# A hybrid attention block: local keys and latents projected transposed, as three pairs of column tiles by seven half-size products

## The chip, the cores and the metric

The kernel runs on one core of a Trainium2 chip. The metric is the device time of one execution in microseconds (us). The engines are PE (matrix products), DVE (element-wise on vectors), ACT (functions, casts and copies), POOL (a further element-wise engine) and SP, which issues most DMA transfers. Each engine works through its own queue in order; semaphores hold an instruction until another engine's result is there. Everything is float32 in and out; products are made in a reduced float32 form, with each operand split into a high and a low part.

## The reference

Per layer (there is one), for 1024 tokens of width 1024:

```python
h  = RMSNorm(x)
p  = h @ w_in    # [SWA q 512 | SWA k 128 | SWA v 128 | q-latent 384 | kv-latent 256 | rope-key 32 | two gates 2048]
A  = sliding_window_attention(rope(q), rope(k), v)        # 8 heads of 64, 2 key heads, window 128
cq, ckv = RMSNorm(q_latent), RMSNorm(kv_latent)
B  = mla_attention(cq @ w_uq, ckv @ w_ukv, rope(rope_key))  # 8 heads, 64 + 32 columns, causal
y  = sigmoid(gate_a) * (A @ w_o_swa) + sigmoid(gate_b) * (B @ w_o_mla)
x  = x + y @ w_out
x  = x + (silu(n @ w_gate) * (n @ w_up)) @ w_down,  n = RMSNorm(x)
return RMSNorm(x)
```

## The kernel before

**Products.** A product of float32 accuracy is three matmuls: high x high, low x high, high x low (`mm3`, L168 to L174). `split` (L161 to L166) makes the parts: ACT casts the high part, DVE subtracts it from the source.

**The normalised input h** comes in blocks of 128 tokens, transposed (`xt`), and is split into four quadrants `hh`, `hl`: two halves of the 1024 features by two halves of the tokens. Each block is also stored to `h_d` in DRAM.

**Projections by block.** For each of eight blocks of tokens there are these products with h as the stationary side: `kvq` (L515), 512 columns: half of the local queries, the local keys, the local values; `qa` (`q_first`, L504), 256 columns: the other half of the queries; later `ql`, 416 columns: the query latents and the rope key; and `kl`, 256 columns: the key-value latents. Rope is applied to queries and keys by `rope_nat` on DVE. Keys must be transposed for the attention: `k_twice`, `k_transposes` (L488) and `k_split` (L497) do it by PE, ACT and DVE. The latents are normalised by row as they come out (`latent_end` L748, `kv_out` L1032), stored to `lat_d`, loaded again behind the local attention (`load_lat` L1076) and transposed there by PE (`latent_T` L1115, forty transposes of 128x128).

**The gates by seven products.** The 2048 gate columns are made by the class `Seven` (L762): two column tiles of 128 by two halves of the tokens by two halves of the features is a 2x2 matrix product, done with seven products of half size (twelve matmuls of 512 columns each) in place of eight. Such products take sums: of the weights (`mix` L802, on POOL in pieces, six operations per pair; plus two for product 7) and of h, called `t1` to `t4`. `set_of_h` (L710) makes these sums for 128 columns of either half of the tokens: loads `hr` and `ht` from `h_d`, DVE does `hr`, POOL `ht` (two operations), DVE `ht` of the other half, ACT and DVE the three splits, and POOL the raw `t4` (two operations, `h`). `prep` (L816) splits the weights of a product, `prep_to` runs it ahead.

**The order.** PE and SP follow the order of the program throughout; up to the local attention ACT, DVE and POOL do too. There the program first interleaves `kvq` and `qa` of the blocks with the normalising of the next, then runs the eight `ql`, beside which the four sets of h are made, then the eight `kl`, beside which the first gate pair is mixed and the `t4` parts are split; then the sixteen steps of local attention with three gate products each. Behind them come the last gate products, the `lT` transposes, and the up-projections `k` and `q` of the latents, for whose weights `uq` and `ukv` are loaded and split there. On-chip buffers are of two kinds of slots, `u` (21) and `v` (17): a tile's transfer waits until the slot's last reader is done.

Of the kernel before, what the change touches and what calls it, by code (L numbers as in the profile page):

```python
# [17 lines left out]
P = 128  # L18
# [24 lines left out]
C_RT = QL  # L43
C_CKV = QL + ROPE_B
LAT = C_CKV + KVL
# [44 lines left out]
def hybrid_block_kernel(  # L90
# [6 lines left out]
    w_qa: bass.AP,  # L97
    w_ql: bass.AP,
    w_kl: bass.AP,
    w_gt: bass.AP,  # L100
    sinks: bass.AP,
    q_g: bass.AP,
    w_uq: bass.AP,
    kv_g: bass.AP,
# [10 lines left out]
    c_rope_b: bass.AP,  # L115
    c_rope_t: bass.AP,
# [80 lines left out]
    rp1 = const.tile([P, 64], F32, name="rp1")  # L197
# [14 lines left out]
    lat_d = dram.tile([NB, P, LAT], F32, name="lat_d")  # L212
# [214 lines left out]
    khd = []  # L427
    for g in range(NG):
        t = V("khd", F32R, (P, 2, S))
        khd.append((t[:, 0], t[:, 1]))  # L430
# [3 lines left out]
    def rope_nat(ps, heads, hw, cos, sin, outs, r=None):  # L434
        n = heads * 2 * hw
        t = U("rp") if heads > 1 else rp1
# [24 lines left out]
    wqa = []  # L461
    kvq_ps, qns, sums, q_ps = {}, {}, {}, {}
# [25 lines left out]
    def k_transposes(b):  # L488
        qn = qns.pop(b)
        nc.sync.dma_start(q_d[NB + b], qn[:, 0:256])  # L490
        pt = kT_ps[b] = P1("kT", (P, NG, P))
        for g in range(NG):
            nc.tensor.transpose(pt[:, g], qn[:, 512 + P * g:512 + P * (g + 1)], ident)

    kT_ps = {}

    def k_split(b):  # L497
        pt = kT_ps.pop(b)
        for g in range(NG):
            nc.scalar.copy(khd[g][0][:, blk(b)], pt[:, g])  # L500
        for g in range(NG):
            sub(khd[g][1][:, blk(b)], pt[:, g], khd[g][0][:, blk(b)].bitcast(F32), nc.vector)

    def q_first(b, mid=None):  # L504
        ps = q_ps[b] = P1("qa", (P, 256))
# [29 lines left out]

    def rope_kvq(b):
        ps = kvq_ps[b]
        r = rn[:, b:b + 1]
        v_hi, v_lo = vv[b // 4][:, b % 4, :, 0:HD], vv[b // 4][:, b % 4, :, HD:P]
        v_ps = ps[:, 384:512].rearrange("p (g d) -> p g d", g=NG)  # L540
        if b < RAW:
            nc.scalar.activation(v_hi, v_ps, AF.Copy, scale=r)
        else:
            nc.scalar.copy(v_hi, v_ps)
        qns[b] = rope_of(ps[:, 0:384], 6, b, r if b < RAW else None)
        if b < RAW:
            nc.vector.scalar_tensor_tensor(v_lo, v_ps, r, v_hi.bitcast(F32), op0=ALU.mult, op1=ALU.subtract)
        else:
            nc.vector.tensor_tensor(v_lo, v_ps, v_hi.bitcast(F32), op=ALU.subtract)
        kvq_ps.pop(b)  # L550

    def k_twice(b):
# [34 lines left out]
    square(1)  # L587
    kvq(2)
    load_xt(5)
    load_xs(5)  # L590
    load_xs(4)
    load_xt(6)
    rope_kvq(0)
    to_quad(3)
    k_twice(0)
    rope_kvq(1)
    to_quad(4)
    square(2)
    k_twice(1)
# [1512 lines left out]
```

## Time and profile before

| | |
|---|---|
| Times of three runs | 1321.82, 1321.95, 1324.46 us (median 1321.95) |
| Span of the profiled execution | 1323.3 us, 19060 instructions |
| Its own time beside the median | 1.35 us above (the span is the only time shown for it) |
| Granted TensorE clock | 9 of 9 in all 40 slices |
| DMA | 245.12 MB, mean 185 GB/s |

A row of a timeline has the start in us, the duration in us (of several alike: from the first start to the last end), engine, line, operation, output <- inputs, shape and count, and in brackets how long the engine had been idle and what ended that. Matmuls are pipelined, so a row's duration is longer than the step from one start to the next; the step is what a stream of them costs.

### The profile page before, as it was taken

How to read it: one execution, taken by the hardware profiler on the slowest of the kernel's cores; microseconds unless marked ns; L12 is line 12 of the kernel's file. 1: busy time of each engine (PE TensorE's matmuls, PEld its weight loads, DVE VectorE, ACT ScalarE, POOL GpSimd, SP SyncE). 2: the span in 40 equal slices, each digit the busy share in tenths (PEclk: the TensorE clock that was granted, in tenths of full speed). 3: DMA queues.
4: the chain of work that ended last, by engine and by line, in shares of the span. 5: the costliest groups of instructions: out<-in, count | busy, mean ns of one | idle time of the engine just before them, and what ended most of it. 6: DMA issues, size and time to landing. Idle time of an engine off the chain costs nothing.

```text
span 1323.3 us, 19060 instructions
## 1 busy us (share of the span) xinstructions
PE 1310.9 (99%) x6516; PEld 1103.7 (83%) x6516; DVE 917.0 (69%) x1517; ACT 634.6 (48%) x1282; POOL 559.0 (42%) x619
## 2 busy tenths in 40 slices
PE   9999999999999999999999999999999999999997
PEld 6899888888888889888888888888888888888886
DVE  6868787786767777777779655656666554664863
ACT  7444667665557666755355232323222223644452
POOL 1116545653324556312232465777567631022521
PEclk9999999999999999999999999999999999999999
DMA  9464344456577477898531334655544435996504
GB/s 359 167 195 154 125 162 145 140 184 212 166 241 201 97 223 160 277 322 195 181 122 48 112 130 172 235 195 206 183 181 148 150 112 198 378 376 224 175 17 142
DMA packets 92192, 245.12 MB, mean 185 GB/s; under 512 B 10304, under 2 KB 17984, under 8 KB 90944
## 3 DMA queue, kind: packets, MB, share of 16 engines
q1 hardware_dynamic: 87264, 233.15, 50.9%
q0 software_dynamic: 3392, 8.39, 3.6%
q10 hardware_dynamic: 1440, 2.36, 0.5%
q8 instruction: 52, 0.85, 0.3%
q14 instruction: 44, 0.36, 0.1%
HBM read 161.16 MB, written 78.51 MB: 181 GB/s over the span
## 4 chain that ended last, share of the span: by engine, by line
PE 63%; DVE 2%; issue 1%; POOL 1%; ACT 1%; POOLq 0%; DVEq 0%; ACTq 0%
PE fa L174 6%; PE fa L172 6%; PE fa L173 6%; PE fd L173 5%; PE fd L172 5%; PE fd L174 5%; PE fb L173 5%; PE fb L174 5%; PE fb L172 5%; PE xo L174 2%; PE xo L172 2%; PE xo L173 2%; PE pTb L1280 1%; PE oB L174 1%; PE oB L172 1%
## 5 line engine op out<-in xcount | busy, mean ns | idle before, releaser
L166 DVE TENSOR_TENSOR wl<-wr,wl 128x512 fp32r<-128x512 f32 x150 | 142.5, 973 | 74.7 <-ACT wl L163 74.2
L166 DVE TENSOR_TENSOR lrv<-lr,lrv 128x1024 fp32r<-128x1024 f32 x77 | 105.5, 1401 | 48.2 <-ACT lrv L163 45.6
L163 ACT CAST lrv<-lr 128x1024 fp32r<-128x1024 f32 x77 | 80.2, 1054 | 90.4 <-PE fd L174 56.7
L172 PE MATMUL fd<-lrv 128*128 128x512 f32 x308 | 119.8, 389 | 0.0
L173 PE MATMUL fd<-lrv 128*128 128x512 f32 x308 | 119.8, 389 | 0.0
L174 PE MATMUL fd<-lrv 128*128 128x512 f32 x308 | 119.8, 389 | 0.0
L177 POOL TENSOR_TENSOR wr<-wr,sm 128x512 f32<-128x512 f32 (+1 forms) x38 | 45.5, 1208 | 139.9 <-DVE wl L166 121.7
L163 ACT CAST wl<-wr 128x512 fp32r<-128x512 f32 x150 | 86.7, 621 | 4.8 <-DVE t3l L177 2.8
L166 DVE TENSOR_TENSOR wl<-sm,wl 128x512 fp32r<-128x512 f32 x60 | 50.2, 859 | 42.1 <-ACT wl L163 41.9
L1265 POOL TENSOR_TENSOR denb<-denb,neg_one 128x1 f32<-128x1 f32 x64 | 39.8, 622 | 92.7 <-ACT p L1264 80.7
L172 PEld LDWEIGHTS fd<-lrv 128*128 128x128 f32 x308 | 57.8, 188 | 12.1
L174 PEld LDWEIGHTS fd<-lrv 128*128 128x128 f32 x308 | 57.8, 188 | 12.0
L173 PEld LDWEIGHTS fd<-lrv 128*128 128x128 f32 x308 | 57.8, 188 | 11.9
L1264 ACT ACTIVATE p<-scb,nmb 128x384 f32<-128x384 f32 (+3 forms) x64 | 47.7, 746 | 32.0 <-DVE nmb L1263 23.5
L361 POOL TENSOR_SCALAR ms<-ss 128x1 f32<-128x1 f32 x32 | 8.9, 278 | 125.9 <-ACT xn L1742 47.5
L1263 DVE CUSTOM_DVE_ANT_0 scb<-scb,mask 128x384 f32<-128x384 f32 (+3 forms) x64 | 48.5, 761 | 17.2 <-PE scb L1255 14.6
L1638 ACT ACTIVATE act<-sm 128x512 f32<-128x512 f32 x11 | 7.0, 635 | 102.1 <-DVE sm L180 102.1
L166 DVE TENSOR_TENSOR ptl<-pTb,pth 128x512 fp32r<-128x512 f32 (+2 forms) x96 | 50.0, 550 | 7.9 <-ACT pth L163 7.7
L163 ACT CAST pth<-pTb 128x512 fp32r<-128x512 f32 (+2 forms) x96 | 43.4, 480 | 18.1 <-PE pTb L1280 17.1
L1266 POOL TENSOR_SCALAR p<-p,denb 128x384 f32<-128x384 f32 (+3 forms) x64 | 48.2, 753 | 6.3
L172 PE MATMUL fa<-t1h,wl 128*128 128x512 f32 x120 | 47.1, 392 | 0.4 <-ACT wl L163 0.4
L172 PE MATMUL fb<-t2h,wl 128*128 128x512 f32 x120 | 47.1, 392 | 0.0
(357 smaller groups left out, 4260.7 us busy)
## 6 DMA issues: line engine op xcount, KB each, us to landing
lr<-la_d SPq DMA_DIRECT2D x77, 256.0 KB, 5.4
wr<-in_w_gate_dram SPq DMA_DIRECT2D x22, 512.0 KB, 4.3
wr<-in_w_up_dram SPq DMA_DIRECT2D x22, 512.0 KB, 5.0
la_d<-sd SPq DMA_DIRECT2D x22, 512.0 KB, 5.2
wd<-in_w_down_dram SPq DMA_DIRECT2D x22, 512.0 KB, 6.6
rb_d<-wd SPq DMA_DIRECT2D x22, 512.0 KB, 2.7
lr<-rb_d SPq DMA_DIRECT2D x44, 256.0 KB, 5.4
lr<-in_w_down_dram SPq DMA_DIRECT2D x33, 256.0 KB, 5.4
```

The lines of the kernel that those rows point to most:

```text
L163: i = nc.scalar.copy(hi, src)
L166: (eng or nc.vector).tensor_tensor(lo, src, hi.bitcast(F32), op=ALU.subtract)
L172: nc.tensor.matmul(ps, ah, bh, start=first and i == 0, stop=False, skip_group_check=go_on)
L173: nc.tensor.matmul(ps, ah, bl, start=False, stop=False, skip_group_check=go_on)
L174: nc.tensor.matmul(ps, al, bh, start=False, stop=last and i == n - 1, skip_group_check=go_on)
L177: eng.tensor_tensor(out, a, b, op=ALU.subtract)
L361: nc.gpsimd.tensor_scalar(ms, ss, 1.0 / width, EPS, op0=ALU.mult, op1=ALU.add)
L1263: nc.vector.tensor_tensor_reduce(s_, s_, m_, 1.0, -NEG, op0=ALU.add, op1=ALU.min, accum_out=nm)
L1264: nc.scalar.activation(p_, s_, AF.Exp, scale=-1.0, bias=nm, accum_out=den)
L1265: nc.gpsimd.tensor_tensor(den, den, neg_one[:, 0:1], op=ALU.pow)
L1266: nc.gpsimd.tensor_scalar(p[:, 0:w], p[:, 0:w], den, 0.0, op0=ALU.mult, op1=ALU.add)
L1280: nc.tensor.transpose(pp[:, i], p[:, blk(k0 + i)], ident)
```

## The change

- The `kvq` product of a block now holds all 512 query columns. The values and the rope key, 160 columns, are a second product `vk`. `qa`, `ql` and `kl` are gone, and so are `k_twice`, `k_transposes` and `k_split`.
- Six column tiles (the local keys, three of query latents, two of key-value latents) are made transposed, features on partitions and tokens along the columns, as three pairs A, B, C by class `Seven`: 21 products of twelve matmuls, with h as the moving side, run as A1, B1, A2, B2, C1, C2, A6, B6, A7, B7, A5, B5, A4, B4, A3, B3, C6, C7, C5, C4, C3. The weights of a pair are first scaled by the norm's gain on ACT (`scale_part`, four operations per half).
- The four sets of h are made earlier, in the order 1, 2, 3, 0, among the last `vk` and the first of these products. The mixes of A, B and C are on POOL between them.
- The keys are given their rope in the transposed form, stored to `ks_d` and loaded twice into `khd`.
- Query latents are stored to `ct_d` with the gain but without the row's norm; the norm `rlat` goes into the attention's scores as a scale. The key-value latents stay on chip (`klr`) until the sums of squares are there, and are normalised within the first five steps of the local attention (`lat_stats`, `lat_diag`, `lat_norm`: 16 `st` and 8 `rb` matmuls of fp32), then stored to `ct_d`.
- Behind the local attention five tiles of 1 MB come back from `ct_d` in place of eight of 0.34 MB; the `lT` transposes are gone, those of the rope key stay.

On POOL, before, beside the `ql` products (`ht`, `h`: sums of h; `ms`, `rstd`: norms of the latents):

```order
L177 TENSOR_TENSOR ht_999<-ht_999 128x256 x2
L177 TENSOR_TENSOR h_164_1083<-hr_998,ht_999 128x256 x2
L361 TENSOR_SCALAR ms_1104<-ss_1102 128x1
L364 TENSOR_TENSOR rstd_1106<-ms_1104,neg_half 128x1
L361 TENSOR_SCALAR ms_1156<-ss_1154 128x1
L364 TENSOR_TENSOR rstd_1158<-ms_1156,neg_half 128x1
L177 TENSOR_TENSOR ht_1109<-ht_1109 128x256 x2
L177 TENSOR_TENSOR h_164_1083<-hr_1108,ht_1109 128x256 x2
```

In the changed kernel on POOL, from the second half of mix A (`sm` and `wr_661`) to the first operation of mix B:

```order
L177 TENSOR_TENSOR sm_891<-wr_661,wr_705 128x256
L174 TENSOR_TENSOR sm_891<-sm_891,wr_661 128x256
L174 TENSOR_TENSOR wr_661<-wr_661 128x2x128
L174 TENSOR_TENSOR ht_755<-ht_755 128x256 x2
L174 TENSOR_TENSOR h_133_931<-hr_754,ht_755 128x256 x2
L174 TENSOR_TENSOR ht_789<-ht_789 128x256 x2
L174 TENSOR_TENSOR h_133_931<-hr_788,ht_789 128x256 x2
L177 TENSOR_TENSOR sm_1011<-wr_707,wr_758 128x256
```

The mix of the first pair now stands between the sums of set 1 and those of set 2 (`ht_755`), and that of the second between set 3 and set 0. On ACT, before, in the same stretch (`wh`: the `kl` weights; `lat`: a square of latents):

```order
L500 CAST khd_164<-kT_1028 128x128
L500 CAST khd_165<-kT_1028 128x128
L231 ACTIVATE wh_1035<-wr_945,gT 128x256 x4
L936 ACTIVATE lat_1045,ss_1046<-ql_1002 128x384
L163 CAST t1h_1081<-hr_998 128x4x128
L163 CAST t3h_1079<-ht_999 128x4x128
L163 CAST t2h_1077<-ht_999 128x4x128
L936 ACTIVATE lat_1101,ss_1102<-ql_1052 128x384
```

In the changed kernel on ACT, from the weights of product B2 (`wl_972`) over set 3 to those of C1 (`wl_1008`) and to set 0:

```order
L160 CAST wl_972<-wr_758 128x512
L160 CAST t1h_870<-hr_788 128x4x128
L160 CAST t3h_868<-ht_789 128x4x128
L160 CAST t2h_866<-ht_789 128x4x128
L918 ACTIVATE wr_929<-wr_929,gT 128x256 x4
L761 COPY pu_1006<-fa_993 128x512
L160 CAST wl_1008<-wr_929 128x512
L160 CAST t1h_870<-hr_925 128x4x128
L160 CAST t3h_868<-ht_926 128x4x128
L160 CAST t2h_866<-ht_926 128x4x128
```

The weights of the next product now stand behind the casts of a set of h, with their scaling in between; for A2 (`wl_954`) and C2 it is the same with sets 2 and 0. The diff, cut to its core:

```diff
-    for j in range(2):
-        plain(("qa", j), w_qa[:, 4 * j:4 * j + 4], (P, 4, 256), True, 4 * j)
-    for j in range(4):
-        plain(("ql", j), w_ql[:, 2 * j:2 * j + 2], (P, 2, 416), False, 2 * j)
-    for j in range(2):
-        plain(("kl", j), w_kl[:, 4 * j:4 * j + 4], (P, 4, KVL), False, 4 * j)
+    plain(("vk", 0), w_vk[:, 0:6], (P, 6, VK), True, 0)
+    plain(("vk", 1), w_vk[:, 6:8], (P, 2, VK), False, 6)
...
-    def k_transposes(b):
-        qn = qns.pop(b)
...
+    def vk(b, mid=None):
+        ps = vk_ps[b] = P1("vk", (P, VK))
+        pairs = [(hT(k, blk(b)), tuple(w[:, k % 6] for w in wvk[k // 6])) for k in range(NK)]
         mm3(ps, pairs[:4], last=False)
         if mid is not None:
             mid()
         mm3(ps, pairs[4:], first=False)
 
+    def vk_out(b):
+        ps = vk_ps.pop(b)
+        v_hi, v_lo = vv[b // 4][:, b % 4, :, 0:HD], vv[b // 4][:, b % 4, :, HD:P]
+        v_ps = ps[:, 0:P].rearrange("p (g d) -> p g d", g=NG)
+        nc.scalar.copy(v_hi, v_ps)
+        nc.vector.tensor_tensor(v_lo, v_ps, v_hi.bitcast(F32), op=ALU.subtract)
+        nc.scalar.copy(kr[:, 0, b], ps[:, P:VK])
...
+    LT = {(0, 0): 4, (0, 1): None, (1, 0): 0, (1, 1): 1, (2, 0): 2, (2, 1): 3}
...
+    def load_lt(j, kh):
+        t = U("wr", F32, (P, 4, 2, P))
+        nc.sync.dma_start(t, w_lt[j, kh])
+        return {"l": t}
+
+    def scale_lt(j, kh, k, raw):
+        t = raw["l"]
+        nc.scalar.activation(t[:, k], t[:, k], AF.Copy, scale=gT[:, 4 * kh + k:4 * kh + k + 1])
...
+    def hi_lo_out(c, sh, src, g=None):
+        t = U("cs", F32R, (P, 2, 512))
+        if g is None:
+            split(t[:, 0], t[:, 1], src)
+        else:
+            nc.scalar.activation(t[:, 0], src, AF.Copy, scale=g)
+            nc.vector.scalar_tensor_tensor(t[:, 1], src, g, t[:, 0].bitcast(F32), op0=ALU.mult, op1=ALU.subtract)
+        lat_stores.append((ct_d[c][:, :, half(sh)], t.bitcast(F32)))
...
+    A, B, C = 0, 1, 2
+    lat_head = [(A, 1), (B, 1), (A, 2), (B, 2), (C, 1), (C, 2), (A, 6), (B, 6), (A, 7), (B, 7), (A, 5), (B, 5), (A, 4),
+                (B, 4), (A, 3), (B, 3)] + [(C, q) for q in (6, 7, 5, 4, 3)]
+    lat = Seven(3, "l", load_lt, lat_done, 1, (1, 6), 5, lat_head, scale=scale_lt, piece=2)
+
+    def lat_run(ahead):
+        lat.run()
+        lat.prep_to(ahead)
...
+    vk(5)
+    h_out(4)
+    q_out(6)
+    load_set(3)
+    nc.sync.dma_start(lg, c_rope_b)
+    vk_out(3)
+    vk(6)
+    lat.scale_part(A, 1)
+    for nm, q in (("b11", (0, 0)), ("b21", (1, 0)), ("b22", (1, 1))):
+        hq[nm] = quad[q]
+    lat.prep_to(1)
+    vk_out(5)
+    rope_q(7)
+    vk(7)
+    lat.scale_part(B, 0)
+    set_of_h(1, nothing)
+    vk_out(6)
+    lat.prep_to(2)
+    lat.mix(A)
+    vk(4)
+    q_out(7)
+    load_set(0)
+    lat.load_part(C, 0)
+    set_of_h(2, nothing)
+    vk_out(7)
+    vk_out(4)
+    quad.clear()
+    lat.scale_part(B, 1)
+    lat.prep_to(3)
+    lat_run(4)
+    lat.load_part(C, 1)
+    set_of_h(3, nothing)
+    lat.scale_part(C, 0)
+    lat_run(5)
+    lat.mix(B)
+    set_of_h(0, nothing)
+    lat_run(6)
+    lat.scale_part(C, 1)
+    lat_run(7)
+    lat_run(8)
+    flush()
+    for sh in (1, 0):
+        rope_k[sh] = U("tk", F32, (P, 2, 512))
+        nc.sync.dma_start(rope_k[sh], c_rope_k[sh])
+    lat_run(9)
...
+    lat.mix(C)
+    lat_run(12)
+    t4_of_h(2)
+    lat_run(13)
+    t4_of_h(3)
+    lat_run(14)
...
+        khd.append(V("khd", F32R, (P, 2, S)))
+        for u in range(2):
+            nc.sync.dma_start(khd[g][64 * u:64 * u + 64].bitcast(F32), ks_d[g].rearrange("a p x c -> (a p) x c"))
...
+    def lat_stats():
+        ps = P1("st", (P, 2 * NB))
+        for grp in range(2):
+            for b in range(NB):
+                t = sqs[(grp, b // 4)][:, b // 4, blk(b % 4)]
+                nc.tensor.matmul(ps[:, NB * grp + b:NB * grp + b + 1], t, neg_one[:, 0:1], start=True, stop=True)
+        for grp, width in ((0, QL), (1, KVL)):
+            c = slice(NB * grp, NB * grp + NB)
+            nc.vector.tensor_scalar(rlat[:, c], ps[:, c], -1.0 / width, EPS, op0=ALU.mult, op1=ALU.add)
+        nc.gpsimd.tensor_tensor(rlat, rlat, neg_half_w, op=ALU.pow)
...
+    lat_tail = {0: lat_stats, 1: lat_diag, 2: lambda: lat_norm(0), 3: lambda: (flush(), lat_norm(1)), 4: flush}
...
-    def latent_T(c0, dst, s):
-        pt = P1("lT", (P, 4, P), F32R)
-        for j in range(4):
-            nc.tensor.transpose(pt[:, j], lat[4 * s + j][:, c0:c0 + P], ident_r)
-        pt = pt.bitcast(F32)
-        split(dst[0][:, half(s)], dst[1][:, half(s)], pt.rearrange("p b c -> p (b c)"))
...
+    def load_ct(c):
+        t = V("ct", F32R, (P, 2, S))
+        nc.sync.dma_start(t.bitcast(F32), ct_d[c])
+        lat_t.append((t[:, 0], t[:, 1]))
+
+    krt = U("krt", F32R, (P, NB, ROPE_B))
+    nc.sync.dma_start(krt.bitcast(F32), kr_d)
+    for c in range(3, 5):
+        load_ct(c)
...
-        nc.vector.tensor_tensor_reduce(s_, s_, m_, 1.0, -NEG, op0=ALU.add, op1=ALU.min, accum_out=nm)
+        nc.vector.tensor_tensor_reduce(s_, s_, m_, rlat[:, n:n + 1], -NEG, op0=ALU.add, op1=ALU.min, accum_out=nm)
```

More of the change, by code (lines that the diff above doesn't have):

```diff
@@ L42 @@
 C_GATE = 1440
[L43 to L45 removed]
+VK = P + ROPE_B
 HF = NF // 2
@@ new lines, in lat_done @@
+    def lat_done(j, m, ps, f, sh, other):
+        c = LT[(j, f)]
+        if c is None:
+            add(other, ps, other, nc.vector)
+            k_rope(sh, other)
+            return
+        if c >= 3:
+            if c not in klr:
+                klr[c] = U("klr")
+            y = klr[c][:, half(sh)]
+            if other is None:
+                nc.scalar.copy(y, ps)
+            else:
+                add(y, ps, other, nc.vector)
+            square_of(1, sh, y)
+            return
+        if other is not None:
+            add(other, ps, other, nc.vector)
+        y = ps if other is None else other
+        hi_lo_out(c, sh, y, latg[:, c:c + 1])
+        square_of(0, sh, y)
@@ L1155, in hybrid_block_kernel @@
         nc.sync.dma_start(d, t)
-    del lat
     wk, wv = wkv2
```

433 lines of the change are left out of this document (196 added, 237 removed).

## The prediction

> **What bounds the kernel now.** I read the page's busy times first, then what the matmul engine (PE) waited for, then the stretches of 20 us around the projections.
>
> ```profile
> span 1323.3 us, 19060 instructions
> PE 1310.9 (99%) x6516; PEld 1103.7 (83%) x6516; DVE 917.0 (69%) x1517; ACT 634.6 (48%) x1282; POOL 559.0 (42%) x619
> PE kvq L574 <- DMA wr<-in_w_x_dram: 0.9, 1, 0.9
> PE fa L172 <- ACT wl L163: 0.4, 1, 0.4
> ```
>
> PE is busy 99% of the span, and its waits on others are of this size (us in total, times, longest). So two things count: how much PE work is removed, and whether the changed order opens a wait on PE. No later slack gives a wait back. The stretches (PE, PEld, DVE, ACT, POOL, each with its busy us, then the clock, DMA share and GB/s) say which engine works beside PE at present:
>
> ```profile
> 60.00:80.00 20.00, 20.00 (x146) 18.78 (x146) 17.62 (x45) 7.29 (x18) 0.00 (x0) 1.00 0.57 182
> 80.00:100.00 20.00, 20.00 (x109) 19.76 (x108) 10.73 (x24) 8.10 (x21) 5.51 (x8) 1.00 0.68 220
> 100.00:120.00 20.00, 19.93 (x117) 19.60 (x116) 17.67 (x43) 6.26 (x15) 12.47 (x19) 1.00 0.53 172
> 120.00:140.00 20.00, 20.00 (x170) 20.00 (x169) 16.14 (x42) 11.85 (x40) 11.81 (x21) 1.00 0.33 115
> 320.00:340.00 20.00, 19.94 (x117) 16.20 (x116) 15.44 (x27) 13.44 (x27) 0.31 (x1) 1.00 0.74 257
> ```
>
> From 80 to 140 us PE runs `ql` and `kl`, which need weights ready long before; under that cover DVE, ACT and POOL build the sums of h and the first mix. The change takes this cover away: the latents themselves now need sums of h.
>
> **PE work removed and added.** Matmul records overlap, so I price by start to start.
>
> ```profile
> 62.20 0.28 PE L174 MATMUL qa<-wv,hl 128*128 128x256 f32 x1
> 62.32 0.40 PE L172 MATMUL kvq<-wv,hh 128*128 128x512 f32 x1
> 83.86 0.35 PE L172 MATMUL ql<-wh,hh 128*128 128x416 f32 x1
> 84.43 0.38 PE L493 MATMUL kT<-ident_r,qn 128*128 128x128 f32 x2
> 84.56 0.43 PE L172 MATMUL ql<-wh,hh 128*128 128x416 f32 x1
> 84.84 0.35 PE L173 MATMUL ql<-wl,hh 128*128 128x416 f32 x1
> 131.30 0.28 PE L971 MATMUL sc<-khd,qs 128*128 128x128 f32 x1
> 131.97 0.28 PE L971 MATMUL sc<-khd,qs 128*128 128x128 f32 x1
> 319.26 0.39 PE L1019 MATMUL o<-pth,vv 128*128 128x512 f32 x1
> 320.17 0.80 PE L1118 MATMUL lT<-ident_r,lat 128*128 128x128 f32 x8
> 320.81 0.47 PE L172 MATMUL fb<-t2h,wl 128*128 128x512 f32 x1
> 321.12 0.40 PE L173 MATMUL fb<-t2l,wl 128*128 128x512 f32 x1
> ```
>
> 256 columns take 0.12. Three `ql` of 416 columns take 84.43 - 83.86 = 0.57, so 0.19 each. The pair kT takes 0.13 and lengthens the next `ql` by 0.09, together 0.22. Six `sc` of 128 columns take 0.67, so 0.112 each; four of 512 columns take 0.91, so 0.228 each. Eight `lT` take 0.64 and 0.08 on the next.
>
> Removed: qa and kl, 384 x 0.12 = 46.1; ql, 192 x 0.19 = 36.5; eight kT pairs, 1.8; 40 lT in 8 groups, 40 x 0.08 + 8 x 0.08 = 3.8. Together 88.2.
> Added: vk, 192 of 160 columns, between 0.112 and 0.12, nearer the 128-column row: 192 x 0.112 = 21.5 (23.0 at the other end). The 21 half-size products, 252 x 0.228 = 57.5. The 16 `st` and 8 `rb` are not in this trace in that place; by the kT pair at 0.22 they are 5.3, by one `sc` 2.7, and I take 4.8, since each fp32 one is two passes like the pair. Together 83.8. Net -4.4 (-6.5 to -2.4).
>
> **The chain that feeds A2, C1 and C2.** The products start A1, B1, A2, B2, C1, C2. A2 needs a scaled and split weight half, which on ACT stands behind the casts of set 2 of h; those wait for POOL, and POOL does mix A first. Rows for the steps:
>
> ```profile
> 54.01 1.02 DVE L443 TENSOR_TENSOR rp<-kvq,ra 128x384 f32<-128x384 f32 x2
> 55.06 0.36 DVE L449 TENSOR_TENSOR qn<-rp 128x192 f32<-128x192 f32 x1
> 55.61 0.28 DVE L549 TENSOR_TENSOR vv<-kvq,vv 128x128 fp32r<-128x128 f32 x1
> 62.41 0.25 ACT L544 CAST vv<-kvq 128x128 fp32r<-128x128 f32 x1
> ...
> 93.41 0.69 DVE L177 TENSOR_TENSOR hr<-ht,hr 128x512 f32<-128x512 f32 x1 [6.00 <-DMA ht<-h_d]
> 94.23 1.44 POOL L177 TENSOR_TENSOR ht<-ht 128x256 f32<-128x256 f32 x2 [5.98 <-DMA hr<-h_d]
> 95.70 0.62 ACT L163 CAST t3h<-ht 128x512 fp32r<-128x512 f32 x1 [0.95 <-POOL ht L177]
> 95.70 0.69 DVE L177 TENSOR_TENSOR ht<-ht,hr 128x512 f32<-128x512 f32 x1
> 96.31 0.68 DVE L166 TENSOR_TENSOR t1l<-hr,t1h 128x512 fp32r<-128x512 f32 x1
> 96.43 0.62 ACT L163 CAST t2h<-ht 128x512 fp32r<-128x512 f32 x1
> 96.47 2.27 POOL L177 TENSOR_TENSOR h<-hr,ht 128x256 f32<-128x256 f32 x2 [0.81 <-DVE ht L177]
> 96.91 1.23 DVE L166 TENSOR_TENSOR t3l<-ht,t3h 128x512 fp32r<-128x512 f32 x1
> 97.43 1.70 ACT L231 ACTIVATE wh<-wr,gT 128x256 fp32r<-128x256 f32 x4
> 98.07 1.23 DVE L166 TENSOR_TENSOR t2l<-ht,t2h 128x512 fp32r<-128x512 f32 x1
> ...
> 157.14 0.74 POOL L180 TENSOR_TENSOR sm<-wr,wr 128x256 f32<-128x256 f32 x1
> 157.95 1.22 POOL L177 TENSOR_TENSOR sm<-sm,wr 128x256 f32<-128x256 f32 x1
> 161.34 0.74 POOL L177 TENSOR_TENSOR wr<-wr 128x256 f32<-128x256 f32 x1
> ```
>
> One set of h takes 5.9 on DVE (93.41 to 99.30), of which it waits for POOL's `ht` until 95.70; POOL is done with its `h` after 5.3. `t3l` and `t2l` take 1.23 instead of 0.69 while POOL runs `h`. A mix of six operations takes 157.14 to 162.08, 4.9.
>
> On before's clock: the seventh kvq starts at 62.32; four qa of 24 become vk (-0.8), five kT pairs before it are gone (-1.1), and it lasts 24 x 0.228 = 5.5. So vk5 runs 65.9 to 68.6, vk6, vk7, vk4 follow at 2.7 each to 76.7, A1 (12 x 0.228 = 2.74) to 79.4, B1 to 82.2. A2 is due at 82.2.
>
> - DVE stands at the split of vk5's v: hi 0.25, lo 0.28, to 69.2. Query rope of 512 columns, 4/3 of the 384 rows (1.36 + 2 x 0.48): 71.5. Set 1 to 77.4 on DVE, 76.8 on POOL.
> - Mix A on POOL to 81.7, `ht` of set 2 to 83.2. DVE's `ht` 83.9, ACT's t2h 84.6, four small copies of vk7 and vk4 85.6, scaling (four of 256) 87.3, cast 87.9. **A2 waits 5.7.**
> - A2 ends 90.6, B2 93.3. Its split lets set 3 begin at 89.8: `hr` 90.5, `ht` 91.9, DVE `ht` 92.6, t2h 93.2, scaling 94.9, copy and cast 96.1. C1, due 93.4, **waits 2.7** and ends 98.8.
> - POOL's `h` of set 3 to 94.9, mix B to 99.8, `ht` of set 0 to 101.2, t2h 102.6, copy and square 103.8, scaling 105.5, cast 106.1. C2, due 98.9, **waits 7.2.**
>
> With 0.2 each for the low halves, the waits come to 16. Shorter end: `h` at 1.44, the mixes at 6 x 0.74, casts at their start-to-start: 12. Longer end: every mix operation at 1.22, as the second is beside DVE: 2 x 2.4 more, 21. From C2 on, preparation runs five products ahead, and ACT's three operations of 0.62 per product fit in 2.74.
>
> A rule that speaks against the change. The first eight matmuls of the kernel show a slow start:
>
> ```profile
> 1.24 3.60 PE L562 MATMUL warm<-warm 128*128 128x512 bf16 x8 [1.24 <-DVE warm L559]
> ```
>
> That is 0.45 each against 0.228 later. If A2 and C2 ran at that pace, each would take 2.7 more; A2's is swallowed, because C1 waits for ACT until 96.1 anyway, C2's is not: +2.7. No wait of such a length stands in this trace after the start. The Trainium skill (TensorE: Matmul & The Clock Gate, "What's actually happening") says that about 3.4 us of idleness halve the array's clock until about 3.4 us of work have passed; by that a wait would cost 1.7 more (an estimate).
>
> **The rest.** Early blocks: DVE loses a kT split and a 256-column rope per block and gains the wider rope; PE covers it, and without cover it is under 1 us. SP's queue: the set loads stand ahead of C's weights, and the store of the seventh queries holds them until about 73.8; C's first half then waits for set 1's buffer (76.8) and is needed at 93.2, so 16 us cover it. The keys go through DRAM to `khd` (1 MB out, 2 MB back, 9 us at the 347 GB/s below) under six products, 16 us. The latents' normalisation goes beside the first attention steps, on a POOL that is busy 42% of the span; without that cover its eight POOL operations of 128 columns, at 0.74 or less, are up to 6. The score's scale operand is the same instruction, on a DVE that idles 31% of the span. All these at 0.
>
> After the windows' end the latents come back as five transfers of 1.05 MB; three need buffers that come free only about 319 to 320, ahead of 1.8 MB of weights. At 257/0.74 = 347 GB/s these 4.9 MB take 14, so the weights land about 334.5 and split by 338.5:
>
> ```profile
> 338.32 1.89 DVE L166 TENSOR_TENSOR wv<-wr,wv 128x512 fp32r<-128x512 f32 x3
> ```
>
> Before, the last split ended at 340.2, and PE arrives 3.8 sooner without `lT`: a wait of 0 to 2.1 at equal slack, more if the transfers collide with stores, up to 4. I take 1.
>
> **Sum.** -4.4 + 16 + 1 = +12.6. The profiled execution's span, 1323.3, lies 1.35 above the median of the runs, 1321.95; I add to the median: **1334.6**.
>
> **Rivals.**
> 1. *PE stays fed, faster.* The place is POOL's queue: from vk5's end to C2's due time PE offers 3 x 2.7 + 5 x 2.74 = 21.8, and C2's chain holds 3.6 of POOL-free start, four `ht`, three `h`, two mixes (22.4) and 4.9 of tail, 30.9. It turns once POOL's steps take under 13.3, as they would at DVE's 0.69 for a 512-column operation (seven of `ht` and `h`, 4.8, and two mixes of three, 4.1: 8.9). Then 1322 - 4.4 + 1 = 1318.6. Against it: ACT's t3h started at 95.70, right when POOL's 1.44 ended, so POOL's spans are real here. 0.15.
> 2. *Half the waits.* Only 4 to 7 of them remain, if casts and POOL overlap better than in the rows: about 1323. 0.07.
> 3. *The pace falls after the waits:* +2.7, 1337.3. For it: the first row of the kernel; against: no such wait is on record. 0.15.
> 4. *The reload of the latents decides:* 4 instead of 1, 1337.6. For it: DMA is at 0.74 there already; against: ACT and DVE have lost the `lT` splits. 0.10.
>
> The forecast keeps 0.53.
>
> **Range and chances.** About 0.2% (2.6 us) can be told from no change. The forecast's own range is 1330 to 1340 (12 to 21). With rivals 2 to 4 it goes from 1320 to 1342 and leaves out rival 1 and little above. Faster 0.15, same 0.07, slower 0.78 (0.53 + 0.15 + 0.10).
>
> **What would show it.** Right: PE waiting about 6 before the third `fa` product, 3 before the fifth, 7 before the sixth, each released by ACT's `wl`, ACT by POOL's `ht`, POOL busy with `sm`; 192 vk at 0.112. Wrong: under 3 us of waits between vk4 and C2; or waits elsewhere, before `k` after the windows, or in the first attention steps; or products after A2 at twice 0.228.

## The result, and the profile after

| | before | after |
|---|---|---|
| Median of the runs | 1322.65 us (four runs, 1321.82 to 1324.46) | 1386.72 us (four runs, 1383.58 to 1389.3) |
| Profiled execution, its span | 1323.3 us | 1381.7 us (its time is 1383.58 us) |
| Granted TensorE clock, mean | 0.999 | 0.978 |

The ratio is 1.0474 (95% interval 1.045 to 1.0499): 64 us slower, where the forecast said 12.6 and its range ended at 20. The two traced spans lie only 58.4 apart: the traced execution after is the shortest of its four, 3.1 under their median, and the one before is longer than its median. What follows explains these 58.4.

The page after: the span, the engines' busy times, then PE's busy tenths and the granted clock in 40 slices.

```profile
span 1381.7 us, 18730 instructions
PE 1322.0 (96%) x6376; PEld 1100.3 (80%) x6376; DVE 931.2 (67%) x1463; ACT 642.1 (46%) x1271; POOL 586.7 (42%) x627
...
PE   9964789999999999999999999999999999999997
...
PEclk9987889999999999999999999999999999999999
```

PE's idle time was 1323.3 - 1310.9 = 12.4 before and is 1381.7 - 1322.0 = 59.7 now. So 47.3 of the 58.4 us between the two spans are waits, and 11.1 are more busy time, although 140 matmuls have gone. The slices put both in the same place, 69 to 207 us. The waits of PE (us in total, times, longest):

```profile
PE fa L169 <- ACT pu L761: 18.2, 3, 8.8
PE qT L818 <- DMA qn<-q_d: 11.6, 1, 11.6
PE fb L169 <- ACT t4h L160: 11.5, 1, 11.5
PE fa L169 <- ACT wl L160: 2.6, 2, 2.1
PE q L169 <- ACT wuq L160: 2.1, 1, 2.1
```

The stretches that answer to those of before (PE, PEld, DVE, ACT, POOL busy, clock, DMA share, GB/s):

```profile
80.00:100.00 20.00, 8.92 (x25) 6.50 (x24) 11.45 (x15) 10.13 (x23) 12.01 (x14) 0.66 0.00 0
100.00:120.00 20.00, 12.88 (x45) 10.07 (x44) 6.30 (x8) 7.37 (x14) 5.12 (x7) 0.74 0.15 53
120.00:140.00 20.00, 8.47 (x30) 6.55 (x29) 9.88 (x15) 6.46 (x11) 10.28 (x11) 0.74 0.17 59
```

From 80 to 140 PE was busy for 59.93 of 60 us before and is for 30.27 now. No engine is full there: DVE, ACT and POOL are each busy for a quarter to 60% of a stretch. They wait for one another in turn, which no engine's total shows. And the clock falls to 0.66. The waits of PE one by one, in the timeline, with the first matmuls behind A2's (the row's bracket: idle before, and what ended it):

```profile
89.54 0.80 PE L169 MATMUL fa<-hh,wl 128*128 128x512 f32 x1 [8.82 <-ACT pu L761]
90.14 0.63 PE L170 MATMUL fa<-hl,wl 128*128 128x512 f32 x1
90.56 0.63 PE L171 MATMUL fa<-hh,wl 128*128 128x512 f32 x1
...
96.40 0.79 PE L169 MATMUL fa<-hh,wl 128*128 128x512 f32 x1 [2.26 <-ACT pu L761]
...
100.82 0.39 PE L169 MATMUL fa<-hh,wl 128*128 128x512 f32 x1
...
110.85 0.80 PE L169 MATMUL fa<-hh,wl 128*128 128x512 f32 x1 [7.12 <-ACT pu L761]
133.66 0.77 PE L169 MATMUL fb<-t3h,wl 128*128 128x512 f32 x1 [11.53 <-ACT t4h L160]
157.29 0.50 PE L169 MATMUL fa<-hh,wl 128*128 128x512 f32 x1 [2.14 <-ACT wl L160]
176.45 0.50 PE L818 MATMUL qT<-ident_r,qn 128*128 128x128 f32 x2 [11.60 <-DMA qn<-q_d]
198.31 3.63 PE L1132 MATMUL st<-neg_one,sq 128*128 128x1 f32 x32
392.85 0.50 PE L169 MATMUL q<-ct,wuq 128*128 128x512 f32 x1 [2.09 <-ACT wuq L160]
```

Two things are to be seen. PE stops at two of the three places that the forecast worked out: before A2 (89.54), 8.8 against 5.7, and before C2 (110.85), 7.1 against 7.2. The third wait between them, 2.3 at 96.40, isn't C1's. Each product is twelve matmuls, so the one that starts at 96.40 is B2, and C1 follows it at 100.82 without a gap. Beside these stand four more: A7 (133.66), B3 (157.29), the first transposed queries `qT` and, behind the local attention, `q`. And after a wait the matmuls start 0.42 to 0.43 apart (90.14 to 90.56) instead of the 0.228 that such a stream took before, for 8 to 14 matmuls. A2 takes 93.98 - 89.54 = 4.44 instead of 2.74, 1.7 more. Counted in the same way it is 1.7 at B2, 2.9 at C2 (the pace stays low into A6), 1.8 at A7, 1.7 at B3, 2.5 behind `qT`, 1.8 behind the 32 one-column matmuls at 198.31, where PE counts as busy, and 1.7 at `q`: 15.8 together. So PE's own work is 11.1 - 15.8 = -4.7, against the forecast's -4.4, and the 58.4 are 47.3 of waits, 15.8 of half pace and these -4.7.

**Who is late, by place.** A2 first: ACT's rows up to the reading of A1's product (`pu`).

```profile
86.00 0.19 ACT L497 COPY kr<-vk 128x32 f32<-128x32 f32 x1 [2.28 <-DVE vv L496]
...
86.72 0.19 ACT L497 COPY kr<-vk 128x32 f32<-128x32 f32 x1 [0.36 <-DVE vv L496]
86.80 1.70 ACT L918 ACTIVATE wr<-wr,gT 128x256 f32<-128x256 f32 x4
88.40 0.60 ACT L160 CAST wl<-wr 128x512 fp32r<-128x512 f32 x1
88.91 0.58 ACT L761 COPY pu<-fa 128x512 f32<-128x512 f32 x1
```

The forecast had the small copies done by 85.6; ACT's copy of the rope key waits 2.28 for DVE's low half of the values. And A2 adds onto A1's accumulator, so it also waits until ACT has copied A1's product out (88.91), which stands behind A2's own weights. B2 waits in the same way for the copy of B1's product, which stands on ACT behind the casts of set 3 and the scaling of C's weights:

```profile
94.18 1.70 ACT L918 ACTIVATE wr<-wr,gT 128x256 f32<-128x256 f32 x4
95.79 0.56 ACT L761 COPY pu<-fa 128x512 f32<-128x512 f32 x1
96.26 0.62 ACT L160 CAST wl<-wr 128x512 fp32r<-128x512 f32 x1
```

The cast of C1's weights, next on ACT, ends at 96.88, well before C1 starts at 100.82: C1 doesn't wait. At C2 the copy of C1's product is what comes last (ACT's rows, and DVE's half of C2's weights):

```profile
107.63 0.68 ACT L938 ACTIVATE cs<-fa,latg 128x512 fp32r<-128x512 f32 x1
107.76 0.69 DVE L163 TENSOR_TENSOR wl<-wr,wl 128x512 fp32r<-128x512 f32 x1 [1.21 <-ACT wl L160]
...
109.20 0.60 ACT L926 ACTIVATE sq<-fa 128x512 f32<-128x512 f32 x1 [0.89 <-DVE cs L939]
109.70 0.61 ACT L160 CAST wl<-sm 128x512 fp32r<-128x512 f32 x1
110.21 0.59 ACT L761 COPY pu<-fa 128x512 f32<-128x512 f32 x1
```

C2's weights were cast by ACT when DVE's half of them began (107.76), and split at 108.45 (107.76 and 0.69), but the copy of C1's product stands behind B2's results and A6's weights. The chain before A7, on ACT and DVE, then ACT's two rows before B3 and SP's rows ahead of `qT`, from the timeline:

```profile
122.16 0.69 ACT L938 ACTIVATE cs<-fa,latg 128x512 fp32r<-128x512 f32 x1 [9.26 <-PE fb L171]
126.74 0.60 ACT L930 ACTIVATE sqt<-fa 128x512 f32<-128x512 f32 x1 [3.89 <-DMA ct_d<-cs]
128.77 0.62 ACT L160 CAST wl<-wr 128x512 fp32r<-128x512 f32 x1 [1.44 <-POOL sq L177]
129.42 1.23 DVE L163 TENSOR_TENSOR wl<-wr,wl 128x512 fp32r<-128x512 f32 x1 [5.79 <-ACT wl L160]
130.58 1.81 DVE L1067 TENSOR_TENSOR kr<-kr,lg 128x256 f32<-128x256 f32 x2
...
132.83 0.68 DVE L177 TENSOR_TENSOR pu<-fb,pu 128x512 f32<-128x512 f32 x1
...
156.10 0.62 ACT L160 CAST ks<-kc 128x512 fp32r<-128x512 f32 x1 [4.29 <-DVE kc L177]
156.62 0.61 ACT L160 CAST wl<-wr 128x512 fp32r<-128x512 f32 x1
...
163.29 2.42 SPq L1094 DMA_DIRECT2D khd<-ks_d  x4
...
166.40 1.08 SPq L810 DMA_DIRECT2D qn<-q_d  x2
```

A square (`sqt`) waits for a store (`ct_d<-cs`) that it doesn't read: the two tiles share a buffer. The `u` slots are all held, and one goes in series through B6's weights, C2's `cs`, its store, `sqt`, the sum on POOL, and A7's weights. Then the rope of the rope key, 2.3 us on DVE, stands ahead of the reading of A6's product (132.83), onto which A7 adds. The bracket of A7's row names ACT's `t4h`, which A7 doesn't read; DVE's reading ended at 133.51, just ahead of A7's start at 133.66, and e2's bracket names it. B3's weights (156.62) stand on ACT behind the cast of the rotated keys, for which ACT had waited 4.29 for DVE's rope; no experiment takes this wait away. The last two rows are SP's: the four transfers of the keys back to `khd`, 512 KB each, stand ahead of the first two of the queries.

### The profile page after: what moved, and what is told of

The parts are those of the page before. It is cut to its first block, busy times and chain, and to the rows that moved or that the text cites. A ratio compares the mean times of both kernels' runs of the same rounds, so it can differ in the third digit from the quotient of the medians.

```text
span 1381.7 us, 18730 instructions
## 1 busy us (share of the span) xinstructions
PE 1322.0 (96%) x6376; PEld 1100.3 (80%) x6376; DVE 931.2 (67%) x1463; ACT 642.1 (46%) x1271; POOL 586.7 (42%) x627
## 4 chain that ended last, share of the span: by engine, by line
PE 62%; issue 1%; POOL 1%; DVE 1%; ACT 0%; POOLq 0%; DVEq 0%
PE fa L171 6%; PE fa L169 6%; PE fa L170 6%; PE fd L170 5%; PE fd L171 5%; PE fd L169 5%; PE fb L170 4%; PE fb L171 4%; PE fb L169 4%; PE xo L171 2%; PE xo L170 2%; PE xo L169 2%; PE pTb L1348 1%; PE oB L171 1%; PE oB L170 1%
## 5 line engine op out<-in xcount | busy, mean ns | idle before, releaser
L163 DVE TENSOR_TENSOR wl<-wr,wl 128x512 fp32r<-128x512 f32 x165 | 156.0, 967 | 87.1 <-ACT wl L160 86.6
L174 POOL TENSOR_TENSOR wr<-wr,sm 128x256 f32<-128x256 f32 (+1 forms) x44 | 50.7, 1165 | 137.9 <-DVE wl L163 122.4
L160 ACT CAST wl<-wr 128x512 fp32r<-128x512 f32 x165 | 95.6, 619 | 9.0 <-DVE t3l L174 2.8
L163 DVE TENSOR_TENSOR wl<-sm,wl 128x512 fp32r<-128x512 f32 x66 | 55.4, 860 | 42.7 <-ACT wl L160 41.3
L169 PE MATMUL fa<-hh,wl 128*128 128x512 f32 x132 | 56.6, 429 | 21.6 <-ACT pu L761 18.2
L169 PE MATMUL fb<-t3h,wl 128*128 128x512 f32 x132 | 53.5, 405 | 11.5 <-ACT t4h L160 11.5
L1331 DVE CUSTOM_DVE_ANT_0 scb<-scb,mask,rlat 128x384 f32<-128x384 f32 (+3 forms) x64 | 52.1, 819 | 13.4 <-PE scb L1323 13.4
L171 PE MATMUL fa<-hh,wl 128*128 128x512 f32 x132 | 55.2, 418 | 0.2 <-DVE wl L163 0.2
L170 PE MATMUL fa<-hl,wl 128*128 128x512 f32 x132 | 54.9, 416 | 0.0
L170 PE MATMUL fb<-t3l,wl 128*128 128x512 f32 x132 | 53.1, 402 | 0.0
```

The source lines that it names most:

```text
L160: i = nc.scalar.copy(hi, src)
L163: (eng or nc.vector).tensor_tensor(lo, src, hi.bitcast(F32), op=ALU.subtract)
L169: nc.tensor.matmul(ps, ah, bh, start=first and i == 0, stop=False, skip_group_check=go_on)
L170: nc.tensor.matmul(ps, ah, bl, start=False, stop=False, skip_group_check=go_on)
L171: nc.tensor.matmul(ps, al, bh, start=False, stop=last and i == n - 1, skip_group_check=go_on)
L174: eng.tensor_tensor(out, a, b, op=ALU.subtract)
```

## The experiments

The theory: each wait is a chain on ACT, DVE, POOL or SP in which something stands ahead that could come later, and each wait costs some 2 us more for the pace. The rivals: one common cause (POOL's sums), or PE's own work. The times of before beside these kernels have medians of 1322.65 to 1323.9, and the ratios are against them.

**e1: the queries' loads ahead of the keys' reload.**

```diff
+    sw_q(0)
+    sw_q(1)
     for g in range(NG):
         khd.append(V("khd", F32R, (P, 2, S)))
...
     flush()
-    sw_q(0)
-    sw_q(1)
```

> The two loads of the first queries are issued ahead of the reload of the keys; nothing else changes. Theory of separate causes: PE's wait of 11.6 us before the first qT is a place in SP's queue, so it falls under 2 us, the twelve matmuls behind it are back at full pace (2.5 us), and the time goes from 1386.7 to about 1373. Rival, the keys themselves are late: they land only at 170 to 175 us, so the wait moves to the first sc and the time stays above 1382.

1384.36 us, ratio 1.0459 (1.0442 to 1.0475). The wait of `qT` went, and another came (the last row is PE's, the others are DVE's ahead of it):

```profile
170.37 1.13 DVE L784 TENSOR_SCALAR wr<-wr,gT 128x256 f32<-128x256 f32 x4
171.60 0.69 DVE L177 TENSOR_TENSOR sm<-wr,wr 128x512 f32<-128x512 f32 x1
172.33 0.69 DVE L174 TENSOR_TENSOR sm<-sm,wr 128x512 f32<-128x512 f32 x1
172.94 0.69 DVE L174 TENSOR_TENSOR wr<-wr 128x512 f32<-128x512 f32 x1
173.54 0.68 DVE L177 TENSOR_TENSOR pu<-fb,pu 128x512 f32<-128x512 f32 x1
174.37 0.77 PE L169 MATMUL fb<-t3h,wl 128*128 128x512 f32 x1 [9.63 <-DVE pu L177]
```

C7 waits for the reading of C6, which stands behind the scaling and the sums of the first gate pair. It had been hidden behind the queries. The expectation missed: a wait was taken away, a second one under it came out.

**e5: e1, and the first gate pair behind the reading of C6.**

```diff
     lat_run(18)
     flush()
-    gates.prep_to(1)
     lat_run(19)
-    gates.mix(0, nc.vector)
...
     sw_qT(0)
+    gates.prep_to(1)
     lat_run(21)
     flush()
+    gates.mix(0, nc.vector)
     gates.prep_to(2)
```

> As e1, and the first gate pair's scaling and mix on DVE stand behind the reading of product C6 instead of ahead of it. In e1 the wait of 9.6 us before C7 was released by that reading, which stood behind them. If so, both the place of the query loads in SP's queue and the place of the gate's mix in DVE's queue held PE at the same point, and only both together free it: no wait over 2 us between C6 and the first steps of the local attention, about 1372.5 from 1386.7. Rival, keys or DVE's load are the bound there: a wait of 5 us or more before the first sc, time above 1380.

1377.1 us, ratio 1.041 (1.0395 to 1.0426). The wait before C7 fell from 9.63 to 4.12, not to nothing. What is left is a third layer: the `cs` of B3, the weights' splits and the sums go back and forth between ACT and DVE, each of which waits for the other (DVE's row `cs` at 167.29 waited 0.85 for ACT, the split of 165.15 waited 1.21).

**e2: buffers of their own for the two `cs`, for `sqt` and for A7's weights.** Two free `v` tiles take the place of the `u` slots in that chain.

```diff
+    own.extend([V("own", F32, (P, 4, 512)) for _ in range(2)])
+    own2.append(own[1][:, 2])
...
-        t = U("sqt", F32, (P, 512))
+        t = own2.pop() if own2 else U("sqt", F32, (P, 512))
...
-        t = U("cs", F32R, (P, 2, 512))
+        t = own.pop().bitcast(F32R)[:, 0:2] if own else U("cs", F32R, (P, 2, 512))
```

> Two 8 KB buffers that are free until the keys are reloaded take the two first stored latents, one square and the weights of product A7, which in the changed kernel share one 4 KB slot with the weights of B2 and B6. Theory of separate causes: PE's wait of 11.5 us before A7 comes from that one slot; it falls under 1 us, the nine half-paced matmuls behind it go (1.8 us), and the time goes to about 1373.5. Rival, the engines that prepare products are overloaded: the wait reappears before B7 or A5 and the time stays above 1382.

1375.24 us, ratio 1.0392 (1.0377 to 1.0408), by the ratios 11 us under the changed kernel. A7 now:

```profile
124.99 0.47 PE L169 MATMUL fb<-t3h,own 128*128 128x512 f32 x1 [2.53 <-DVE pu L177]
```

The shared slot was 9 us of A7's 11.5, and with the wait its half pace went too. That is shown; the remaining 2.5 end with DVE's reading of A6, ahead of which the rope stands.

**e3: mix A and mix B on POOL behind all four sets of h.**

```diff
     lat.prep_to(2)
-    lat.mix(A)
...
     lat_run(5)
-    lat.mix(B)
...
     lat.scale_part(C, 1)
+    lat.mix(A)
+    lat.mix(B)
```

> Mix A and mix B stand behind all four sets of h in POOL's queue. Theory of the prediction (set 2 and set 0 wait for a mix): the wait before A2 falls from 8.8 to about 5, that before C2 from 7.1 to about 4.8, C1 keeps 2.3, A6 is just in time: about 1380.5. Rival, POOL's throughput is the bound: what A2 and C2 gain is lost before A6 and B6, and the time stays above 1385.

1380.4 us, ratio 1.0429 (1.0411 to 1.0446). The time is what the theory said, the waits only in part: A2 waits 6.0 instead of 8.8, where about 5 was expected, and C2 6.4 instead of 7.1, where 4.8 was. So POOL's order is about a third of A2's wait, and a small part of C2's.

**e4: unread matmuls of 512 columns before A2, C1, C2, A7 and qT (36, 9, 30, 48, 49).** They are meant to keep PE busy while it waits. The nine before C1 stand where PE doesn't wait; ahead of B2 there are none.

```diff
+    def fill(n):
+        t, w = PX("dm"), hq["b11"][0][:, 0]
+        for _ in range(n):
+            nc.tensor.matmul(t, w[:, 0:P], w, start=True, stop=True)
...
+    fill(36)
     lat_run(6)
```

> Before A2, C1, C2, A7 and the first qT PE runs 36, 9, 30, 48 and 49 matmuls of 512 columns whose result nobody reads, so that it is not idle while it would wait. Theory of the clock gate: the matmuls after these places run at 0.228 instead of 0.427; of the 14 us lost to half pace those before A2 and C1 are swallowed by the next wait, 7 come off the time, about 1379.5. Rival, the pace has another cause than idleness: still 0.427 there, and no time gained (1386 or more).

Ratio 1.0427 (1.0409 to 1.0444), three executions from 1378.23 to 1381.95; one of 4802.85 is left out. Its stretch from 80 to 100:

```profile
80.00:100.00 20.00, 15.46 (x63) 12.08 (x62) 11.49 (x15) 10.02 (x24) 11.92 (x14) 0.95 0.01 5
```

The clock is 0.95 there instead of 0.66, and the run is 6.2 us faster (by the ratios, 0.0047 of 1322.65) although PE does 172 matmuls more. A2, C2, A7 and the products behind `qT` start 0.22 to 0.24 apart there; B2, which waits 3.83 with nothing filled in, still runs at half pace. So the pace is a cost of its own beside the waits, and it comes from PE standing still, not from the products.

**e6: e2, e3 and e5 together, and the rope of the rope key behind the reading of A6.** No other edit.

> The edits of e2, e3 and e5 together, and the rope key's rotation on DVE behind the reading of A6. If the waits have separate causes, the gains add: 11.5 (e2) + 6 (e3) + 14 (e5) + 2 (the 2.5 left before A7 in e2), about 1353 from 1386.7. Rival, one overloaded chain: they do not add, time above 1365.

1364.51 us, ratio 1.0316 (1.0299 to 1.0333). That lies between the two theories. Alone, the three edits had brought 10.8 (e2), 6.0 (e3) and 8.5 (e5) by the ratios, 25 together, where 14 had been put down for e5; e6 brings 21. With intervals of 2 to 3 us on each, this doesn't show whether the gains add. What is left: C2 still waits 4.75, A2 6.02, C7 3.98, and B7, behind A7, 1.88.

**e7: the same in another order.** Set 1 of h ahead of the last `vk`, the copy of the rope key ahead of the low half of the values, both halves of C ahead of sets 3 and 0, mix A behind set 2, mix B within set 0; the first query weights loaded ahead of three of the five latents; the `st` in two groups. Its core:

```diff
-    set_of_h(3, nothing)
     lat.scale_part(C, 0)
     lat_run(5)
-    lat.mix(B)
-    set_of_h(0, nothing)
+    set_of_h(3, nothing)
     lat_run(6)
+    set_of_h(0, nothing, lambda: lat.mix(B))
```

> As e6, but set 1 of h stands ahead of the last values and queries, where DVE was idle, C1's and C2's weights are prepared ahead of sets 3 and 0, mix A stands behind set 2 and mix B behind set 0's first half; the rope key's copy no longer waits for the low half of the values; the sums of squares come in two groups of eight; the first query weights are loaded ahead of three latents. If the order alone makes the waits, those before A2 and C1 fall under 1 us and C2 under 2, A6 and B6 take up to 5 together: about 1335. Rival, DVE and POOL cannot make four sets and two mixes in the time whatever the order: the waits of together 13 us in e6 come back before A6 and B6, time above 1345.

1354.13 us, ratio 1.024 (1.022 to 1.0259). That is the rival's time, and not at the place it named: A2, B2 and C1 don't wait at all, and then C2 does, for C1's copy:

```profile
101.13 0.80 PE L169 MATMUL fa<-hh,wl 128*128 128x512 f32 x1 [12.38 <-ACT pu L763]
```

That copy stands on ACT behind the casts of set 0 (e9 moves it). The 2.1 before `q` are gone; 1.8 before `k` are there in their place.

**e8: the changed kernel with the copy of C1 ahead of the weights of A6 and B6.**

```diff
-    lat_run(7)
-    lat_run(8)
+    lat.run()
+    lat.run()
+    lat.prep_to(8)
```

> The changed kernel with one thing moved: the reading of C1's accumulator (ACT's pu) is emitted ahead of the weights of A6 and B6, so on ACT it stands only behind what B2 leaves. Theory: C2 waits for that reading and not for its own weights, which were ready at 107.73 while it started at 110.85; C2 now starts near 108.2, its wait falls from 7.1 to about 4.5, and the run comes to about 1384.1. Rival: the weights of A6, now behind the reading, are late in their turn and A6 waits for what C2 no longer does: 1386.5 or more.

1385.02 us, ratio 1.0466 (1.045 to 1.0482), not to be told from the changed kernel. In the trace the copy starts at 109.00 and C2 at 109.63, 13.94 behind the start of B2 instead of 14.45. Only 0.5 came of it. C2's own wait is even longer, 8.20: B2 waits only 1.38 here and runs at full pace, so C1 ends earlier. The reason for the 0.5: ahead of the copy stand B2's `cs` and `sq`, and ACT waits there for DVE.

**e9: e7 with the readings of B2 and C1 ahead of set 0.**

```diff
     lat_run(6)
-    set_of_h(0, nothing, lambda: lat.mix(B))
-    lat.scale_part(C, 1)
...
-    lat_run(7)
-    lat_run(8)
+    lat.run()
+    lat.run()
+    set_of_h(0, nothing, lambda: lat.mix(B))
+    lat.scale_part(C, 1)
+    lat.prep_to(8)
```

> The last version (e7, 1354.1) with the readings of B2 and C1 emitted ahead of the last set of sums of h, its casts and mix B, instead of behind them. Theory: in e7 the 12.38 before C2 is one copy of an accumulator that stands in ACT's row behind that set (C2's weights were ready at 90.65, C1 ended at 88.75); now C2 starts near 91 and ends near 93.5, and A6, which needs the whole of t2, waits until the set is done, near 98.5 to 99.5 instead of 105.7: some 6 us less, 1348. If so, about half of the wait was the order of the readings and half is the set itself, which has no product left to lie beside. Rival: the set on DVE, POOL and ACT, pushed behind the readings, ends as much later, and A6 starts at 103 or after: 1352 or more.

1353.76 us, ratio 1.0221 (1.0198 to 1.0243): the rival's number, with the theory's mechanism in part. The wait of 12.38 split in two:

```profile
93.28 0.76 PE L169 MATMUL fa<-hh,wl 128*128 128x512 f32 x1 [3.76 <-ACT pu L763]
102.20 0.80 PE L169 MATMUL fb<-t2h,wl 128*128 128x512 f32 x1 [4.33 <-ACT wl L160]
```

A6 starts at 102.20 instead of 105.72, but now there are two waits with two stretches of half pace, and by C7 (144.53 instead of 147.00) 2.5 us of it are left; the medians show 0.4, less than the runs can tell apart. With e7 this is the fastest version that computes all of it.

**e10 and e11: without the sums.** e10 leaves out every sum for the 21 products, and the gates read plain quarters of h too; it has the buffers of e2, the places of the query loads and of the gates' mix of e5, that of the rope key's rope of e6, and e7's part within the attention, but the changed kernel's order of the readings. e11 is e9 without the sums of the weights.

> Leaves out, around the 21 new products, every sum and difference that they need: of the latents' weights (mix, and the difference of the seventh product) and of the normalised input (the four sets with their loads, t1 to t4 with their casts); the products read plain quarters instead, the gates' products too, so that all products stay with their number and shape. Queries come ahead of the keys' reload, the cs buffers are their own, and the first query weights and statistics are placed as in e7. Theory: the prediction's term for TensorE's own work stands, and all the rest is preparation that arrives late: no wait over 2.5 left before the attention, 1317 to 1321. Rival: the new order costs TensorE by itself (weights, waits on accumulators, tail): over 1326.

> The version e9 without the sums of the latents' weights alone (mix A, B, C and the difference of the seventh product: 11 of GpSimd's groups of two), with the sets of the normalised input kept. Theory: what is late is the sets of the input, on DVE and ACT, and GpSimd's sums of the weights only stand in between: C2 and A6 still wait, 6 of their 8.1 together, and the run comes to about 1345. Rival: GpSimd's sums are what the sets wait for, and without them the waits before C2, A6 and C7 go: 1335 or less.

1348.44 us, ratio 1.0195 (1.0176 to 1.0213), and 1355.99 us, ratio 1.0242 (1.022 to 1.0264). Neither answers its question: the fifth product read a part of the weights that had been given up by then, so that it was loaded a second time, and C7 stood behind that. In e10:

```profile
139.79 1.14 ACT L160 CAST wl<-wr 128x512 fp32r<-128x512 f32 x2 [10.05 <-DMA wr<-in_w_lt_dram]
```

**e12 and e13: the same with a part that is still there.**

```diff
-                src = self.part(j, m, *{6: (0, 0), 5: (0, 1), 1: (0, 0), 2: (1, 0), 7: (0, 1), 4: (1, 1), 3: (1, 0)}[q])
+                src = self.part(j, m, *{6: (0, 0), 5: (1, 1), 1: (0, 0), 2: (1, 0), 7: (0, 1), 4: (1, 1), 3: (1, 0)}[q])
```

> As e10, every sum of the weights and of the input around the 21 products left out, but the fifth product reads a quarter that is still in SBUF: in e10 it read one that had been given up, each pair of columns loaded it once more, and C7 stood 13.77 behind such a load. Theory: with preparation out of the way the new order costs TensorE no more than its short waits (1.2, 0.5, 2.1, 0.7 and 1.7 in e10, with about 3.5 of half pace behind two of them), and its own work is the 4.4 less that the prediction counted: 1326 to 1331, 18 below e10. Rival: products or waits that no preparation explains: over 1334.

> As e11, the version e9 without the sums of the latents' weights but with the sets of the normalised input, without e11's loads in vain. Theory: e11 less the 14.12 before C7 and the half pace behind it, 1339; so of what e9 loses against e12, GpSimd's sums of the weights would be the larger part. Rival: the sets alone still cost as much as sets and sums: 1350 or more.

e12: 1336.09 us, ratio 1.0091 (1.0074 to 1.0108). e13: 1344.77 us, ratio 1.0155 (1.014 to 1.017). Both lie 5 us or more above what the theories said, e12 above 1334, the rival's bound. Against e9's 1353.76, the sums of the weights are worth 9. Between e13 and e12 lie another 8.7, for the sets of h, though e12 also differs from e13 in the order of the readings. So neither is the one cause. e12's busy times, from the page, and its longest wait, from the timeline:

```profile
PE 1310.3 (98%) x6376; PEld 1092.9 (82%) x6376; DVE 909.2 (68%) x1439; ACT 632.3 (47%) x1255; POOL 544.3 (41%) x587
```

```profile
132.89 0.77 PE L169 MATMUL fb<-hh,wl 128*128 128x512 f32 x1 [4.32 <-DVE pu L177]
```

PE is busy for 1310.3, against 1310.9 before. Half pace is 4.4 of that (2.3 behind C7, 1.7 behind a wait of 1.72 at 212.19, 0.4 in places), so its own work is 5.0 less than before. Its idle time is 1335.5 - 1310.3 = 25.2, 12.8 more than before. So even without any sum this order keeps 12.8 us more of waits than before; the waits listed for its splits of weights and its readings of accumulators come to 10.8, and the first weights, from DRAM, to 1.4 more than before. They would have to go too before the 5 us of PE work could show; whether an order exists that does it was not tried. The products themselves are cheaper; the loss is in what feeds them and in the half pace behind it.

## Why the prediction was wrong

The forecast was slower by 12.6; it came to be 64. By its own steps, in the profiled execution (58.4 between the spans):

- **PE's own work, -4.4:** right. -4.7 by the trace after, -5.0 by e12; the `vk` of 160 columns start 0.111 apart, where 0.112 was taken.
- **The waits before A2, C1 and C2, 16:** the sum is near, 18.2, and that is partly luck. A2 and C2 wait where the forecast has it. C1 doesn't wait; B2's 2.3, which the forecast doesn't have, stands in for C1's 2.7. The step that failed is "A2 ends 90.6, B2 93.3": a second product adds onto the accumulator of its first, so it waits until ACT has read that (`pu`). The forecast has this copy in ACT's row ("copy and cast 96.1") and lets B2 run without it. By the rows, the chain over POOL and ACT to the casts of the weights alone would have held A2 until 89.00, 8.3, and C2 until about 107.75, 4.0; the copies make up the other 5.9, and all three waits end with `pu`, not with `wl` as the forecast wanted to see. A2's chain also held a copy of the rope key that waits 2.28 for DVE, and POOL's mixes were a part of it (e3).
- **"From C2 on, preparation runs five products ahead, and ACT's three operations of 0.62 per product fit in 2.74":** this step failed, with 11.5 before A7 and 2.1 before B3. It counted operations and their time, and left out that each needs a free buffer (e2: 9 us) and what else stands ahead of it on its engine: the rope ahead of A6's reading, the keys' cast ahead of B3's weights. Weights that are ahead in the program's text aren't ahead in time if the slot for them comes free late.
- **"The keys go through DRAM to `khd` ... 9 us ... under six products, 16 us", at 0:** the step failed, with 11.6. The keys themselves were in time (in e5, where no query holds PE, no product waits for them); the cost is in what is queued behind their transfers on SP's queue, the queries. And under it lay C7's own lateness (e1: 9.6), of which 5.5 came from DVE's scaling and sums for the gates (e5, where 4.1 stay).
- **The pace behind waits, 2.7 with a chance of 0.15:** the mechanism was there, its size was wrong: 15.8 at eight places, mostly 1.7 to 1.8 at each. "A2's is swallowed" held, though not by C1: B2 starts when ACT has read B1's product, however fast A2 ran. B2's half pace is swallowed in the same way, as e8 shows, where it is gone and C2 waits 8.20 instead of 7.12. So some 3.4 of the 15.8 cost no time of their own; e4, which takes it away behind C2, A7 and `qT` (7.2 together), gained 6.2.
- **The reload, 1:** 2.1 of wait and 1.7 of half pace. The rival, which gave it 4, was nearer, and e7 shows that moving the weights ahead puts 1.8 before `k` instead.
- **The steps of the normalisation, at 0:** no wait for them is in the trace, but the 32 one-column matmuls bring half pace with 1.8.

The five rows of waits shown for the profile after come to 46.0 of the 47.3; the other 1.3 are in small pieces.

## What to carry to other kernels

Work that is moved under no cover is late once per chain, not once: list every reader and every writer of each accumulator and buffer in the new order, and for each queue what now stands behind the moved step, before setting a term to zero. With PE at 99% of the span, price each new wait with the half pace that follows it, about 1.7 us for this kernel's 512-column products, unless the next wait ends at a time of its own and swallows it. And when a wait is taken out, look at what was late behind it: e1, e5, e7 and e9 each uncovered the next one; in e1 a wait of 11.6 us went, and the time fell by about 2, no more than the noise. When a sum comes out near, count the products in the trace: here a wait stood one product beside the place that the forecast named, for another reason.

## What the runs showed of the hardware

- Behind a wait, 512-column matmuls start 0.427 apart instead of 0.228, for 3 to 6 us. The Trainium skill (TensorE: Matmul & The Clock Gate, "What's actually happening") gives about 3.4 us of idleness as the condition, by a window that runs freely. The length of a single wait doesn't decide it here: 2.26 us before B2 and 1.72 in e12 (212.19) were followed by half pace; 2.53 before A7 in e2, 2.10 in e12 (121.09) and 1.38 before B2 in e8 were not.
- A row of 32 fp32 matmuls of one column each, 3.63 us in which the profile calls PE busy, was followed by half pace as a wait is; what the condition is exactly stays open. e4's fill, matmuls of 512 columns whose results nobody reads, kept the clock at 0.95 where it had been 0.66.
